# Forming the S3 weight sums of a down projection later, from loads of their own

## The chip, the core and the metric

The kernel runs on one core of a Trainium2 chip. The core has TensorE (matmuls into PSUM), VectorE, ScalarE and GpSimd (elementwise work), and SyncE, whose instruction stream here issues nearly all loads. Each engine works through its own instruction stream in order and waits on semaphores of the others. The metric is the device time of one execution in microseconds (us), the median of several runs.

## The reference

One layer of a decoder trunk over 1024 tokens of width 1024. The layer has three token-mixer branches, an output projection, and a gated MLP; a final RMSNorm closes it. The stage that matters here is the end of the MLP:

```
def _ffn(x, w_gate, w_up, conv_w, conv_b, w_down):
    g = _causal_dwconv(x @ w_gate, conv_w, conv_b)
    return (jax.nn.gelu(g) * (x @ w_up)) @ w_down
...
    x = x + g2[:, None, :] * _ffn(xn, f_wgate, f_wup, f_conv_w, f_conv_b, f_wdown)
return _rmsnorm(x, final_norm)
```

The hidden width of the MLP is 2816 = 22 x 128, so w_down has 2816 rows and 1024 columns. All arrays are float32.

## The kernel before

Every large product is done as a 2 x 2 block product with seven block products in place of eight (the Strassen-Winograd scheme), and every float32 operand is split into two float32r parts, high (`wh`, made by ScalarE) and low (`wl`, made by VectorE or GpSimd as source minus high). A block product is then three matmuls for each pair: high x high, high x low, low x high.

**The gate/up stage** comes before the down stage. For each of 11 pairs k of hidden blocks it makes a gate unit and an up unit of seven products each (line 191 issues their matmuls), loading raw weights into a ring of four buffers (`raw`) and splitting them into rings of eight `wh` and eight `wl` tiles. The convolution and the GELU make `y`, the up unit's evacuation (lines 161 to 172) makes `up`, and `down_tokens` multiplies them and stores the result to `ff_scr`, and four sums of its blocks to `ta_scr` to `td_scr`, from ScalarE's queue (lines 1532 to 1545). The tiles `y`, `up` and `gp` lie in pools that are closed when the stage ends; the pool `sums` with the tiles `held` and `held3`, and the pools `dn` and `last`, are opened in the memory that becomes free.

**The down stage** has seven products, listed in `STEPS`, with 11 rows each: B11 x A11, B21 x A12, ta x S1, tb x S2, B22 x S4, tc x S3, td x A22. A12, A21 and so on are the blocks of w_down and S1 = A21 + A22, S2 = S1 - A11, S3 = A11 - A21, S4 = A12 - S2 its sums. A row is one block of 128 hidden channels: a token tile and a weight tile of 128 x 512, loaded into one `raw` buffer of the same ring (`down_load`: 256 KB each), two splits on ScalarE (`high`), two on VectorE (`low`), and 12 matmuls, three for each of four token tiles (`down_mm`, line 1614). The seven products share PSUM banks in turn and are emptied by `copies` (ScalarE) and `adds` (VectorE). `settle` scales a finished quarter by the gate row `g2b` and adds it to the residual tile `res`; `square` sums its squares on ScalarE.

The order of this stage is written out by hand. `at_slot(s, kind, f)` puts a piece of work at a slot; a slot is one row of a product, so product number si has slots 11 si to 11 si + 10. The pieces are sorted by slot and kind and recorded in this order, and each engine keeps the order of its own instructions. A row's load stands `LD` = 5 slots before its matmuls, its high split `HI` = 3, its low split `LO` = 2; what would fall before slot 0 stands at slot 0. The first two rows are loaded earlier, inside the last gate/up unit (`begun`). How the rows of the down stage interleave with the end of the gate/up stage is decided by a scheduler, which goes by a model of the machine.

The sum S3 is needed in the sixth product only, but A11 is loaded in the first. So row k of the first product also loads A21 into `held3[k]` (line 1670), and `third` (line 1699) subtracts it from the A11 in the raw buffer. The residual tiles `res[t]` are loaded at slots 12 + 2 t, and the second product is settled in the four slots behind it.

Of the kernel before, what the change touches and what calls it, by code (L numbers as in the profile page):

```python
# [16 lines left out]
OP = mybir.AluOpType  # L17
# [8 lines left out]
HALF = 512  # L26
# [43 lines left out]
def trunk(ctx: ExitStack, tc: tile.TileContext, I: dict, out: bass.AP, dbg=None):  # L70
    nc = tc.nc
    pe, act, dve, pool = nc.tensor, nc.scalar, nc.vector, nc.gpsimd
# [20 lines left out]
    def rows_scr(name, n):  # L93
        return [dram.tile([P, S], F32, name=f"{name}{k}_scr") for k in range(n)]
# [6 lines left out]
    x2_scr = rows_scr("x2", NT)  # L101
    ff_scr = rows_scr("ff", KF)
    KH = KF // 2
# [15 lines left out]
    def kview(w, c0, n, r0=0, r1=None):  # L119
        return w[r0:r1, c0:c0 + n].rearrange("(k p) c -> p k c", p=P)  # L120

    def raw_tile(view, shape):
        raw = ring.tile([P] + shape, F32, tag="raw", bufs=4, name="raw")
        nc.sync.dma_start(raw, view)
        return raw
# [7 lines left out]
    def ring_tmp(shape):  # L133
        return ring.tile([P] + shape, F32, tag="st", bufs=3, name="st")
# [458 lines left out]
    for h in range(2):  # L593
        for i in range(4):
            t = 4 * h + i
# [771 lines left out]
    for q in range(4):  # L1367
        raw = raw_tile(kview(I["p_c"], 256 * q, 256, CSPLIT * P, W), [KW - CSPLIT, 256])
# [27 lines left out]
    with ExitStack() as gl_s:  # L1396
# [8 lines left out]
        for h in range(2):  # L1405
# [3 lines left out]
            for c in range(2):  # L1409
                cs = slice(HALF * c, HALF * c + HALF)  # L1410
                pts = [pwo.tile([P, HALF], F32, tag="wo", bufs=4, name="go") for _ in range(4)]
                for k in range(KD):
                    if k % 2 == 0:
                        raw = raw_tile(kview(I["w_out"], HALF * c, HALF, k * P, (k + 2) * P), [2, HALF])
# [10 lines left out]
            for i in range(4):  # L1425
                t = 4 * h + i
# [120 lines left out]
    lo, hi = slice(0, HALF), slice(HALF, D)  # L1547
# [8 lines left out]
    def block_rows(n, k):  # L1556
        r0 = (k + KH * (n[2] == "2")) * P
        return I["f_wdown"][r0:r0 + P, hi if n[1] == "2" else lo]

    def down_load(tn, wn, k, raw=None):  # L1560
        raw = ring.tile([P, 2, HALF], F32, tag="raw", bufs=4, name="raw") if raw is None else raw
        nc.sync.dma_start(raw[:, 0], token_rows(tn, k))
        if wn != "S3":
            nc.sync.dma_start(raw[:, 1], block_rows({"S1": "A21", "S2": "A11", "S4": "A12"}.get(wn, wn), k))
        return raw
# [42 lines left out]
    held, held3 = [[sums.tile([P, HALF], F32, tag=n, bufs=KH, name=n) for _ in range(KH)] for n in ("held", "held3")]  # L1608

    def down_mm(bank, ts_, ws, tp, start):  # L1610
        (th, tl), (wh, wl) = ts_, ws
        sl = slice(tp * P, tp * P + P)
        for j, (a_, b_) in enumerate(((th, wh), (th, wl), (tl, wh))):
            pe.matmul(bank, a_[:, sl], b_, start=(start and j == 0), stop=(j == 2), skip_group_check=True)  # L1614

    def four(bk):
        return [gb3("x") if bk == "x" else gb3("zzww"[tp]) for tp in range(4)]
# [3 lines left out]
    res = [dn.tile([P, D], F32, tag="res", bufs=NT, name="res") for _ in range(NT)]  # L1621
# [5 lines left out]
    LD, HI, LO = 5, 3, 2  # L1627
    todo = []

    def at_slot(s_, kind, f):  # L1630
        todo.append((max(0, s_), kind, f))

    def settle(d, t, sl):

        dve.tensor_tensor(d, d, g2b[:, sl], op=OP.mult)
        dve.tensor_tensor(res[t][:, sl], res[t][:, sl], d, op=OP.add)

    def square(t, dh):
        junk = dn.tile([P, HALF], BF16, tag="junk", bufs=2, name="junk")
        act.activation(junk, res[t][:, (lo, hi)[dh]], AF.Square, scale=1.0 / math.sqrt(D),  # L1640
                       accum_out=ms[t][:, dh:dh + 1])
        if dh == 0:
            pool.tensor_scalar(ms[t][:, 0:1], ms[t][:, 0:1], EPS, None, op0=OP.add)
        else:
            pool.tensor_tensor(ms[t][:, 0:1], ms[t][:, 0:1], ms[t][:, 1:2], op=OP.add)
            pool.tensor_tensor(ms[t][:, 0:1], ms[t][:, 0:1], mhalf[:, :1], op=OP.pow)

    def finish(t):
        for dsl in (lo, hi):
            dve.scalar_tensor_tensor(res[t][:, dsl], res[t][:, dsl], ms[t][:, 0:1], fnb[:, dsl], op0=OP.mult,  # L1650
                                     op1=OP.mult)

    def store(t):
        for dsl in (lo, hi):
            nc.sync.dma_start(out[0, t * P:(t + 1) * P, dsl], res[t][:, dsl])

    def row(si, k, need, slot, alone=False):

        _, tn, wn = STEPS[si]
        it = {}  # L1660

        def load():
            if si == 0 and k < len(begun):
                it["raw"] = begun[k]
            elif alone:
                it["raw"] = down_load(tn, wn, k, lp.tile([P, 2, HALF], F32, tag="lraw", bufs=2, name="lraw"))
            else:
                it["raw"] = down_load(tn, wn, k)
            if wn == "A11":
                nc.sync.dma_start(held3[k], block_rows("A21", k))  # L1670
            if wn == "S1":
                nc.sync.dma_start(held[k], block_rows("A22", k))

        def tile_(tag):
            return lp.tile([P, HALF], F32R, tag="last", bufs=4 * ALONE, name="last") if alone else \
                ring.tile([P, HALF], F32R, tag=tag, bufs=8, name=tag)

        def high():
            raw = it["raw"]
            w = raw[:, 1]  # L1680
            if wn == "S3":
                w = held3[k]
            elif wn in ("S1", "S2", "S4"):
                w = held[k]
                x_, op, y_ = {"S1": (raw[:, 1], OP.add, w), "S2": (w, OP.subtract, raw[:, 1]),
                              "S4": (raw[:, 1], OP.subtract, w)}[wn]
                dve.tensor_tensor(w, x_, y_, op=op)
            it["src"] = raw[:, 0], w
            it["h"] = [tile_("wh") for _ in range(2)]
            for h, src in zip(it["h"], it["src"]):  # L1690
                act.activation(h, src, AF.Copy)  # L1691

        def low():
            it["l"] = [tile_("wl") for _ in range(2)]
            for l, h, src in zip(it["l"], it["h"], it["src"]):
                dve.tensor_tensor(l, src, h.bitcast(F32), op=OP.subtract)  # L1696

        def third():
            dve.tensor_tensor(held3[k], it["raw"][:, 1], held3[k], op=OP.subtract)

        if wn == "A11":
            at_slot(need - LO, 2.5 if need <= LO else 2, third)
        at_slot(need - LD, 0, load)
        at_slot(need - HI, 2, high)
        at_slot(need - LO, 2 if need <= LO else 1, low)
        return lambda: [(h, l) for h, l in zip(it["h"], it["l"])]

    banks, cs = {}, {}
# [22 lines left out]
    for si in range(7):  # L1731
        bk = STEPS[si][0]
        for k in range(KH if si < 6 else KH - ALONE):
            slot = si * KH + k
            get = row(si, k, slot, slot)

            def mm(si=si, bk=bk, k=k, get=get):
                fresh = bk not in banks
                if fresh:
                    banks[bk] = four(bk)  # L1740
                ts_, ws = get()
                for tp in range(4):
                    down_mm(banks[bk][tp], ts_, ws, tp, fresh)

            at_slot(slot, 3, mm)
        if si < 6:
            for tp in range(4):
                at_slot(slot, 5, lambda f=evacs[si], tp=tp: f(tp))
        if si in settled:
            c, t0, dh = settled[si]  # L1750
            for tp in range(4):
                t = t0 + tp
                at_slot(slot + 1 + tp, 4, lambda c=c, tp=tp, t=t, dh=dh: settle(cs[c][tp], t, (lo, hi)[dh]))
                at_slot(slot + 2 + tp, 4, lambda t=t, dh=dh: square(t, dh))
                if dh:
                    at_slot(slot + 3 + tp, 4, lambda t=t: finish(t))
                    at_slot(slot + 4 + tp, 4, lambda t=t: store(t))
    alone = [row(6, KH - ALONE + i, end - 6 + 2 * i, end, True) for i in range(ALONE)]

    def last(tp):  # L1760
# [15 lines left out]
    at_slot(6, 0, lambda: nc.sync.dma_start(g2b, bcast_rows(g_rows[5], P, D)))  # L1776
    at_slot(8, 0, lambda: nc.sync.dma_start(fnb, bcast_rows(I["final_norm"], P, D)))
    for t in range(NT):
        at_slot(12 + 2 * t, 0, lambda t=t: nc.sync.dma_start(res[t], x2_scr[t]))
    for _, _, f in sorted(todo, key=lambda x_: x_[:2]):  # L1780
        f()
    sched2.close()
# [23 lines left out]
```

## Time and profile before

| | us |
|---|---|
| median of 3 runs | 1966.98 (1965.74 to 1968.68) |
| the profiled execution | 1959.93 |
| its span on the core | 1958.1 |
| TensorE busy (matmuls) | 1856.8, 95% of the span |
| VectorE busy | 1295.8, 66% |
| ScalarE busy | 912.8, 47% |
| GpSimd busy | 633.3, 32% |

Times in the profile are counted from the start of the span. A matmul's record overlaps the next one's, so a busy TensorE says only that it did not pause; where it does pause, the rows name the instruction that released it. The granted clock is the share of full speed that TensorE was given. The profile calls the engines PE (TensorE), PEld (its weight loads), DVE (VectorE), ACT (ScalarE), POOL (GpSimd) and SP (SyncE); a q behind the name means the engine's instruction queue, where DMAs are issued.

### The profile page before, as it was taken

The page shows a single profiled execution, that of the slowest core. Times are in us where ns is not written, and L with a number is a line of the kernel's source. Part 1 is how long each engine was busy: PE and PEld are TensorE (multiplying, and loading weights), DVE is VectorE, ACT ScalarE, POOL GpSimd, SP SyncE. Part 2 cuts the span into 40 slices and gives each one's busy share as a digit, 9 for nine tenths or more (in the row PEclk, how much of TensorE's full clock was granted, in tenths as well). Part 3 has the DMA queues.
Part 4 walks back from the last instruction along what each step waited for, and adds up shares of the span by engine and source line. Part 5 has one row for each costly group of instructions (what it writes and reads, how often), then busy time and mean ns, then how long its engine had stood idle before and what let it go on. Part 6 is the DMA issues. An engine that isn't in the chain of part 4 may idle for free.

```text
span 1958.1 us, 26389 instructions
## 1 busy us (share of the span) xinstructions
PE 1856.8 (95%) x9119; PEld 1493.1 (76%) x9119; DVE 1295.8 (66%) x2277; ACT 912.8 (47%) x1689; POOL 633.3 (32%) x1067
## 2 busy tenths in 40 slices
PE   6899998999999999899999999998999999979996
PEld 5677897867777788677777777776888887858885
DVE  5766566556767885555666655579758566667766
ACT  5345456665444444644545433445434343434542
POOL 5320000001311211345656654655545444200001
PEclk9899999999999999899999999999999999989998
DMA  9232423434666768867756256404334333189643
GB/s 322 79 108 100 142 98 129 133 120 156 198 188 198 237 228 250 207 156 177 184 150 164 91 205 214 135 22 140 134 102 130 109 125 101 64 287 324 217 154 121
DMA packets 243078, 313.15 MB, mean 160 GB/s; under 512 B 15991, under 2 KB 166755, under 8 KB 242944
## 3 DMA queue, kind: packets, MB, share of 16 engines
q1 hardware_dynamic: 197520, 186.43, 31.3%
q10 hardware_dynamic: 30384, 75.65, 10.2%
q0 software_dynamic: 15040, 49.38, 9.4%
q8 instruction: 72, 1.18, 0.3%
q14 instruction: 62, 0.51, 0.1%
HBM read 229.47 MB, written 81.93 MB: 159 GB/s over the span
## 4 chain that ended last, share of the span: by engine, by line
PE 78%; DVE 7%; ACT 5%; DMA 4%; issue 3%; POOL 2%; ACTq 0%; SPq 0%; DVEq 0%; POOLq 0%
PE g L298 20%; PE g L191 19%; PE g L1614 10%; PE gp L1158 7%; PE g L337 5%; PE go L1420 4%; PE sl L1225 3%; PE g L215 2%; PE tp L1269 1%; PE o L1298 1%; PE gp L1383 1%; PE o L1301 1%; PE m L790 1%; DVE st L252 1%; ACT wh L254 1%
## 5 line engine op out<-in xcount | busy, mean ns | idle before, releaser
L298 PE MATMUL g<-xs,wh 128*128 128x512 f32 x1344 | 437.7, 407 | 12.0 <-ACT ot L161 12.0
L191 PE MATMUL g<-xs,wh 128*128 128x512 f32 x1176 | 367.9, 394 | 9.5 <-DVE up L168 2.7
L298 PEld LDWEIGHTS g<-xs,wh 128*128 128x128 f32 x1344 | 254.3, 191 | 82.1 <-ACT ot L161 13.7
L298 PE MATMUL g<-xs,wl 128*128 128x512 f32 x672 | 269.1, 400 | 0.0
L191 PEld LDWEIGHTS g<-xs,wh 128*128 128x128 f32 x1176 | 220.5, 188 | 63.0 <-DVE up L168 3.1
L191 PE MATMUL g<-xs,wl 128*128 128x512 f32 x588 | 230.4, 393 | 0.0
L1158 PE MATMUL gp<-oT,wh 128*128 128x512 f32 x512 | 171.6, 415 | 7.3 <-DVE ot L170 3.6
L116 ACT ACTIVATE wh<-raw 128x512 fp32r<-128x512 f32 (+2 forms) x163 | 92.9, 586 | 175.2 <-PE g L191 45.3
L254 ACT ACTIVATE wh<-st 128x512 fp32r<-128x512 f32 x120 | 75.6, 630 | 179.9 <-DVE st L252 179.9
L298 PEld LDWEIGHTS g<-xs,wl 128*128 128x128 f32 x672 | 128.7, 192 | 31.5
L117 POOL TENSOR_TENSOR wl<-st,wh 128x512 fp32r<-128x512 f32 x63 | 101.9, 1618 | 144.7 <-ACT wh L116 139.9
L191 PEld LDWEIGHTS g<-xs,wl 128*128 128x128 f32 x588 | 110.5, 188 | 24.9
L1614 PE MATMUL g<-wh 128*128 128x512 f32 x292 | 114.9, 393 | 14.6 <-ACT wh L1691 14.0
L117 POOL TENSOR_TENSOR wl<-raw,wh 128x512 fp32r<-128x512 f32 (+2 forms) x71 | 92.1, 1298 | 103.0 <-ACT wh L116 100.3
L337 PE MATMUL g<-wh,xs 128*128 128x256 f32 x672 | 124.8, 286 | 0.0
L1614 PE MATMUL g<-wl,wh 128*128 128x512 f32 x292 | 114.9, 393 | 0.6 <-DVE wl L1696 0.6
L1614 PE MATMUL g<-wh,wl 128*128 128x512 f32 x292 | 114.4, 392 | 0.0
L116 ACT ACTIVATE wh<-st 128x512 fp32r<-128x512 f32 x84 | 52.5, 628 | 130.4 <-PE g L191 96.4
L1158 PEld LDWEIGHTS gp<-oT,wh 128*128 128x128 f32 x512 | 89.9, 192 | 30.1 <-issue 7.7
L1691 ACT ACTIVATE wh<-raw 128x512 fp32r<-128x512 f32 x102 | 62.6, 628 | 102.1 <-issue 29.8
L1696 DVE TENSOR_TENSOR wl<-raw,wh 128x512 fp32r<-128x512 f32 x102 | 68.8, 689 | 55.6 <-ACT wh L1691 55.2
L337 PEld LDWEIGHTS g<-wh,xs 128*128 128x128 f32 x672 | 103.8, 188 | 1.6 <-issue 1.4
(331 smaller groups left out, 3922.2 us busy)
## 6 DMA issues: line engine op xcount, KB each, us to landing
raw<-in_w_in_dram SPq DMA_DIRECT2D x66, 512.0 KB, 4.9
raw<-in_f_wdown_dram SPq DMA_DIRECT2D x62, 256.0 KB, 4.3
adaw<-in_w_ada_dram SPq DMA_DIRECT2D x48, 256.0 KB, 5.4
g_scr<-ot ACTq DMA_DIRECT2D x24, 512.0 KB, 3.9
adaw<-in_w_ada_dram POOLq DMA_DIRECT2D x48, 256.0 KB, 4.8
raw<-g_scr SPq DMA_DIRECT2D x24, 512.0 KB, 3.5
qk<-k_scr POOLq DMA_DIRECT2D x24, 512.0 KB, 7.3
raw<-in_f_wgate_dram SPq DMA_DIRECT2D x22, 512.0 KB, 3.8
```

The source lines that it names most:

```text
L116: act.activation(h, src, AF.Copy)
L117: l_eng.tensor_tensor(l, src, h.bitcast(F32), op=OP.subtract)
L191: pe.matmul(banks[bk], a[:, k, :], b, start=(fresh and j == 0), stop=(j == 11), skip_group_check=True)
L254: act.activation(it["h"], bl[name], AF.Copy)
L298: pe.matmul(banks[bk], a[:, k, :], b, start=(fresh and j == 0), stop=(j == 11), skip_group_check=True)
L337: pe.matmul(banks[t2][bk][:, 256 * i:256 * i + 256], a[:, sl], b[:, k % 2, :], start=(fresh and i == 0 and j == 0), stop=(j == 11), skip_g ...
L1158: pe.matmul(pt, a_[:, k % g, :], b_, start=(j == 0), stop=(j == 3 * n - 1))
L1225: pe.matmul(sb[:, of:of + n], lq, kt[:, ks], start=(of == 0 and kt is kh), stop=(kt is kl), skip_group_check=True)
L1420: pe.matmul(pt, a_[:, sl], b_, start=(k == 0 and j == 0), stop=(k == KD - 1 and j == 2))
L1614: pe.matmul(bank, a_[:, sl], b_, start=(start and j == 0), stop=(j == 2), skip_group_check=True)
L1691: act.activation(h, src, AF.Copy)
L1696: dve.tensor_tensor(l, src, h.bitcast(F32), op=OP.subtract)
```

## The change

The subtraction that forms S3, and the load of A21 for it, leave the rows of the first product. A new list of 11 pieces does the same later: `third_load(k)` loads A21 into `held3[k]` and A11 once more into a temporary tile (`ring_tmp`, a ring `st` of three buffers that the gate/up stage used too) at slot 7 + 7k // 5, that is slots 7 to 21, and the subtraction on VectorE stands three slots later. The residual loads stand eight slots later, at 20 + 2 t. The settles and squares of the second product stand 12 slots later, at 34 to 38 in place of 22 to 26.

```diff
-            if wn == "A11":
-                nc.sync.dma_start(held3[k], block_rows("A21", k))
...
-        def third():
-            dve.tensor_tensor(held3[k], it["raw"][:, 1], held3[k], op=OP.subtract)
-
-        if wn == "A11":
-            at_slot(need - LO, 2.5 if need <= LO else 2, third)
...
-                at_slot(slot + 1 + tp, 4, lambda c=c, tp=tp, t=t, dh=dh: settle(cs[c][tp], t, (lo, hi)[dh]))
-                at_slot(slot + 2 + tp, 4, lambda t=t, dh=dh: square(t, dh))
+                at_slot(slot + 1 + tp + 12 * (si == 1), 4, lambda c=c, tp=tp, t=t, dh=dh: settle(cs[c][tp], t, (lo, hi)[dh]))
+                at_slot(slot + 2 + tp + 12 * (si == 1), 4, lambda t=t, dh=dh: square(t, dh))
...
+    a11 = {}
+
+    def third_load(k):
+        a11[k] = ring_tmp([HALF])
+        nc.sync.dma_start(held3[k], block_rows("A21", k))
+        nc.sync.dma_start(a11[k], block_rows("A11", k))
+
+    for k in range(KH):
+        at_slot(10 + 7 * k // 5 - 3, 0, lambda k=k: third_load(k))
+        at_slot(10 + 7 * k // 5, 2, lambda k=k: dve.tensor_tensor(held3[k], a11.pop(k), held3[k], op=OP.subtract))
...
-        at_slot(12 + 2 * t, 0, lambda t=t: nc.sync.dma_start(res[t], x2_scr[t]))
+        at_slot(20 + 2 * t, 0, lambda t=t: nc.sync.dma_start(res[t], x2_scr[t]))
```

The changed lines move instructions on four engines. SyncE's queue, from the load of row 1 (raw_15698) on, before; ff0 to ff10 are the token blocks of the first product:

```order
L1562 DMA raw_15698<-ff1_scr_168 128x512 [waits DMAHW4_49,DMAHW2_49,DVE_49]
L1564 DMA raw_15698<-in_f_wdown_dram 128x512 [waits DMAHW3_49]
L1670 DMA held3_15878<-in_f_wdown_dram 128x512 [waits DMAHW2_49,DMAHW3_49,DMAHW1_49,DMAHW4_49,DMAHW0_49,DMAHW5_49,DVE_49,DMAHW6_49,PE_49,DMAHW7_49,Activation_49,Pool_49]
L1670 DMA held3_15879<-in_f_wdown_dram 128x512
L1562 DMA raw_15911<-ff2_scr_169 128x512 [waits Pool_49]
L1564 DMA raw_15911<-in_f_wdown_dram 128x512
L1670 DMA held3_15880<-in_f_wdown_dram 128x512
L1562 DMA raw_15915<-ff3_scr_170 128x512
```

And in the changed kernel, from the same load on:

```order
L1562 DMA raw_15698<-ff1_scr_168 128x512 [waits DMAHW4_49,DMAHW2_49,DVE_49]
L1564 DMA raw_15698<-in_f_wdown_dram 128x512 [waits DMAHW3_49]
L1562 DMA raw_15909<-ff2_scr_169 128x512 [waits DMAHW5_49,DVE_49]
L1564 DMA raw_15909<-in_f_wdown_dram 128x512 [waits DMAHW6_49]
L1562 DMA raw_15912<-ff3_scr_170 128x512 [waits DMAHW7_49,DMAHW3_49,DVE_49]
L1564 DMA raw_15912<-in_f_wdown_dram 128x512 [waits DMAHW4_49]
L1562 DMA raw_15915<-ff4_scr_171 128x512 [waits DMAHW1_49,DMAHW6_49,DMAHW0_49,DVE_49]
```

The load of held3's first tile, which waits for every engine and DMA lane, stood ahead of rows 2 and later; now it stands behind row 12's load.

TensorE's stream around the last group of the gate/up stage (g3_15746) in the changed kernel; wh_15930 is row 1, wh_15938 row 2. Before, this group stood directly behind row 1:

```order
L1614 MATMUL g3_15952<-wh_15930,wl_15933 128x512
L1614 MATMUL g3_15949<-wh_15938,wh_15937 128x512
L1614 MATMUL g3_15949<-wl_15942,wh_15937 128x512 [waits DVE_49]
L1614 MATMUL g3_15949<-wh_15938,wl_15941 128x512
L1614 MATMUL g3_15950<-wh_15938,wh_15937 128x512
L1614 MATMUL g3_15950<-wl_15942,wh_15937 128x512
L1614 MATMUL g3_15950<-wh_15938,wl_15941 128x512
L1614 MATMUL g3_15951<-wh_15938,wh_15937 128x512
L191 MATMUL g3_15746<-xs_12374,wh_15823 128x512 [waits DVE_49]
```

Seven matmuls of row 2 moved ahead of the group.

ScalarE's stream in the last up unit of the changed kernel; raw_15909 is row 2, raw_15912 row 3, raw_15915 row 4. Before, none of these splits stood there; the first of them came behind the stores of L1532 to L1545:

```order
L165 ACTIVATE up_15540<-g3_15705 128x512 [waits PE_49]
L1689 ACTIVATE wh_15938<-raw_15909 128x512 [waits DMAHW6_49,PE_49,Activation_49]
L1525 ACTIVATE y_15693<-y_15693 128x1024 [waits DVE_49]
L1525 ACTIVATE y_15694<-y_15694 128x1024 [waits DVE_49]
L1689 ACTIVATE wh_15945<-raw_15912 128x512 [waits DMAHW3_49,PE_49,Pool_49]
L167 ACTIVATE up_15541<-g3_15705 128x512 [waits DMAHW7_49,PE_49]
L1689 ACTIVATE wh_15946<-raw_15912 128x512 [waits DMAHW4_49,PE_49,Activation_49]
L1689 ACTIVATE wh_15972<-raw_15915 128x512 [waits DMAHW6_49,PE_49,Activation_49]
L1532 DMA ff21_scr_188<-up_15541 128x1024 [waits DVE_49]
```

The splits of rows 2 to 4 moved in among the up unit's evacuations, one of them directly ahead of L167.

## Rows read from the trace of the kernel before

**Rows 1.** The page's slices: the span in 40 equal parts, TensorE and traffic.

```profile
PE   6899998999999999899999999998999999979996
GB/s 322 79 108 100 142 98 129 133 120 156 198 188 198 237 228 250 207 156 177 184 150 164 91 205 214 135 22 140 134 102 130 109 125 101 64 287 324 217 154 121
```

**Rows 2.** Windows of 10 us: length, busy time of five engines, clock, DMA share, GB/s.

```profile
1700.00:1710.00 10.00, 10.00 (x45) 8.26 (x44) 6.65 (x7) 4.68 (x6) 0.00 (x0) 1.00 0.00 0
...
1720.00:1730.00 10.00, 0.00 (x0) 0.00 (x0) 3.84 (x6) 0.00 (x0) 0.00 (x0) 0.58 0.63 216
1730.00:1740.00 10.00, 6.74 (x18) 5.07 (x19) 6.26 (x10) 3.77 (x6) 0.00 (x0) 0.57 0.83 268
1740.00:1750.00 10.00, 10.00 (x46) 8.27 (x45) 8.60 (x14) 5.63 (x9) 0.00 (x0) 1.00 1.03 380
1750.00:1760.00 10.00, 10.00 (x46) 8.29 (x45) 7.99 (x13) 6.67 (x12) 0.00 (x0) 1.00 1.04 393
1760.00:1770.00 10.00, 10.00 (x46) 8.28 (x45) 4.56 (x8) 5.70 (x10) 0.00 (x0) 1.00 0.98 358
1780.00:1790.00 10.00, 10.00 (x46) 8.26 (x45) 7.08 (x12) 4.16 (x8) 0.00 (x0) 1.00 0.98 357
...
1810.00:1820.00 10.00, 10.00 (x46) 8.29 (x45) 8.62 (x14) 5.85 (x11) 0.00 (x0) 1.00 0.90 307
```

**Rows 3.** TensorE's waits from 1690 to 1950: total us, times, longest.

```profile
PE g L1614 <- ACT wh L1691: 14.0, 1, 14.0
PE g L1614 <- ACT up L167: 0.7, 1, 0.7
```

**Rows 4.** TensorE's instructions: start, us, instruction, count, idle time before and its end.

```profile
1718.92 0.39 PE L191 MATMUL g<-xs,wl 128*128 128x512 f32 x1
1733.26 0.79 PE L1614 MATMUL g<-wh 128*128 128x512 f32 x1 [13.96 <-ACT wh L1691]
...
1738.42 0.47 PE L1614 MATMUL g<-wh,wl 128*128 128x512 f32 x1
1738.73 0.40 PE L1614 MATMUL g<-wh 128*128 128x512 f32 x1
```

**Rows 5.** Waits of SyncE's queue from 1600 to the end.

```profile
SPq L1562 <- DVE wl L1696: 96.0, 57, 5.2
SPq L1670 <- DMA ff_scr<-up: 49.9, 2, 44.1
```

**Rows 6.** The chain that ended last, in order of time: start, us, what.

```profile
1723.98 2.70 DMA td_scr<-y
...
1726.76 0.33 SPq L1670
...
1733.26 179.54 PE g L1614 x779
```

**Rows 7.** VectorE's instructions that read the raw buffers for the last time.

```profile
1681.81 0.69 DVE L148 TENSOR_TENSOR st<-raw,st 128x512 f32<-128x512 f32 x1 [1.87 <-POOL wl L117]
...
1689.60 0.69 DVE L117 TENSOR_TENSOR wl<-raw,wh 128x512 fp32r<-128x512 f32 x1
...
1697.11 0.68 DVE L1696 TENSOR_TENSOR wl<-raw,wh 128x512 fp32r<-128x512 f32 x1
```

**Rows 8.** DMA issues from 1725 to 1760: count, KB each, median us to landing.

```profile
raw<-ff_scr SPq DMA_DIRECT2D x16, 256.0 KB, 5.3
raw<-in_f_wdown_dram SPq DMA_DIRECT2D x15, 256.0 KB, 5.5
```

**Rows 9.** ScalarE's copy L167 in the last up unit.

```profile
1712.24 0.60 ACT L167 ACTIVATE up<-g 128x512 f32<-128x512 f32 x1 [1.31 <-PE g L191]
```

**Rows 10.** One turn of the down stage's loop on ScalarE, VectorE and SyncE.

```profile
1768.66 1.15 ACT L1691 ACTIVATE wh<-raw 128x512 fp32r<-128x512 f32 x2 [1.57 <-PE g L1614]
1769.33 1.29 DVE L1696 TENSOR_TENSOR wl<-raw,wh 128x512 fp32r<-128x512 f32 x2 [1.42 <-ACT wh L1691]
1770.65 0.32 SPq L1562 DMA_DIRECT2D raw<-ff_scr  x1
1771.01 0.43 SPq L1564 DMA_DIRECT2D raw<-in_f_wdown_dram  x1
```

## The prediction, made before the result was known

> **What bounds the kernel now.** I read the slices of the page first, then the stretch that looked odd in windows of 10 us, then who waited for whom there, and last the chain that ended last. In the slices the reader is to see that TensorE is nearly full between the first and the last slice, except in slice 36 of 40, where its digit is 7, next to the highest traffic of the program (324 GB/s) [rows 1]. In windows this is the start of the down stage: between 1720 and 1730 us TensorE executes nothing, between 1730 and 1740 it is busy for 6.74 us with a granted clock of 0.57, and from 1740 on it never pauses [rows 2]. The waits name it: one wait of 14.0 us of TensorE for ScalarE's split of a loaded row, and only 0.7 us of another kind beside it [rows 3]. The instructions give the exact size: the last matmul of the gate/up stage starts at 1718.92, the next one at 1733.26, and twelve matmuls from there stand further apart than later [rows 4].
>
> Why did the split wait? Its row had not been loaded, and SyncE's queue shows why: it stood 44.1 us behind one DMA of L1670, the load of A21 into held3 [rows 5]. That load writes into memory that the gate/up stage's y and up tiles had held, so it waits for their last stores; in the chain its issue follows at once on the td_scr store at 1726.7 [rows 6]. All loads of rows 2 to 10 stood behind it, though they need nothing of that memory. After the start the chain is 779 matmuls of L1614 without a gap [rows 6]. So what is lost before 1733 is lost at the end of the program, as long as nothing later waits longer.
>
> **The change part by part.** A slot is one row of the down stage: 12 matmuls. From 1738.73 on the chain's matmuls take (1733.26 + 179.54 - 1738.73) / 767 = 0.227 us each [rows 4, 6], so a slot is 2.72 us.
>
> *What goes.* The held3 loads leave the head of SyncE's queue. Rows 2 and 3 then need only free buffers of the raw ring, which the last up unit releases: its S4 sum at 1681.81 + 0.69 and its A22 split at 1689.60 + 0.69 [rows 7]. So they can be issued at about 1682.5 and 1690.3, and with the 5.5 us to landing that the loads took while the DMA engines were full [rows 8] they are there by 1696, long before TensorE comes to them; 1700 to 1710 had no DMA traffic at all [rows 2]. Row 4 follows when row 0 is split (1697.11 + 0.68 [rows 7]). What that removes:
> - the idle stretch, 1733.26 - (1718.92 + 0.227) = 14.11 us;
> - the slow matmuls behind it: 12 in 1738.73 - 1733.26 = 5.47 us where 12 x 0.227 = 2.72 would do, so 2.75 us. They run at the lower of the two clocks (1.2 GHz) after an idle stretch; without it there is no reason for the clock to fall.
>
> *What is late next.* I followed the new order through the last up unit by these durations. The order moves a piece of row 2 ahead of the last L191 group, and on ScalarE row 3's first split stands ahead of L167, the copy that frees a PSUM bank for the fourth part of row 0. Both wait for the same L191 group, so L167 ends about 0.6 us (one ScalarE pass [rows 9]) later than 1712.84, and the matmul that waited 0.7 us for it waits some 1.25 us: a loss of 0.55 us. Behind it: row 0's rest, row 1 and 7 matmuls of row 2 (22 in all) to 1718.5, the last L191 group to 1721.2, row 2's rest to 1722.3, then row 3, 4, 5. Row 5's last split, on the buffer that the last L191 group frees at 1721.2, ends near 1722.5 and is wanted at 1727.7; rows 6 and 7 have their loads by 1720 and their splits by 1728, and are wanted at 1730.4 and later. Row 3 starts at 1722.3 instead of 1738.73: 16.4 us, the same as 14.11 + 2.75 - 0.55 = 16.3.
>
> *What is added.* Eleven loads of A11, 256 KB each, and the eleven of A21 moved from the first slots to slots 7 to 21. On SyncE an issue takes 0.32 to 0.43 us [rows 10] and the queue mostly waits for VectorE's splits [rows 5], so 11 more cost nothing there. The eleven subtractions are the same ones as before, 0.69 us each on VectorE, moved from slots 0 to 10 into slots 10 to 24, where VectorE was busy for 4.56 us of 10 in the window from 1760 [rows 2] and the settles of the second product (two passes a tile) have left: nothing, as long as their loads are there. The third-last of them (row 8) now stands directly ahead of the four adds that empty the PSUM banks which the third product needs; by the loop below it ends about as TensorE delivers the first of these, with some 1 us to spare. The residual loads go to slots 20 to 34 and are first wanted at slot 34, 14 slots on. The settles and squares of the second product go to slots 34 to 37: for those four slots VectorE has five passes (about 3.2 us by the pace of [rows 7]) a slot of 2.72 us, a backlog of 2 us against splits that are made two slots, 5.4 us, ahead.
>
> *The unknown is the DMA traffic of slots 7 to 27.* The rows there need 13.9 MB, the new pairs 5.8 MB, four residual tiles 2.1 MB and the broadcast norm row 0.5 MB: 22.3 MB in 21 x 2.72 = 57.2 us, 390 GB/s. The windows show up to 393 GB/s at a full share, 358 with residual tiles in the mix, and 307 in the slowest window with a share of 0.90 [rows 2]. What lateness can be borne is in the loop: ScalarE starts a split when TensorE frees its buffer (1768.66), VectorE is done with it at 1770.62 and the load into the freed raw buffer goes out at 1770.65 [rows 10]. That load is for a row whose own split starts four slots after 1768.66, so it has 10.9 - 2.0 = 8.9 us to land, 3.4 more than the 5.5 us seen; and a split that ends 2 us after its start is used three slots after it, so 6.2 us more pass before TensorE waits. Together 9.5 us. Adding up slot by slot what is asked and what a rate delivers, the loads fall behind by at most 3.1 us at 393 GB/s and 5.8 us at 358: hidden. At 307 it is 16.8 us, so a stall of 7.3 us, with one slow start of 2.75 us about 10. I take the value nearest to the rows with a share of 0.98 and above, which is nothing, and keep 10 for the range. A gain from this part is excluded, since it only adds bytes.
>
> On this the rows show 380 and 393 GB/s over 10 us each, on one core [rows 2]. The Trainium skill (DMA: Bandwidth & Descriptors, Specifications) gives a limit of about 358 GB/s for one core from HBM. By that figure the loads would be 5.8 us late at most and the sum would still be 16.3; by the rows the limit lies higher. It speaks against the change in one way: it leaves 3.7 us of cover and not 6.4.
>
> **Sum.** 14.11 + 2.75 - 0.55 = 16.3 us. Against the profiled execution, 1959.9 us (span 1958.1 and 1.8 around it), that gives 1943.6. The median of the timed runs, 1967.0, lies 7.0 above the profiled one, spread over what the trace can't show, so I subtract the same from it: 1950.7 us.
>
> **The rivals.**
> 1. *The loads of slots 7 to 27 come late.* For it: the 390 GB/s asked is what the fullest windows gave, and held3's subtractions stand in VectorE's order ahead of splits and of the adds that free PSUM banks. Against it: before, these engines moved 358 to 393 GB/s with TensorE never waiting [rows 2, 3]. At 307 GB/s the gain is 16.3 - 10 = 6.2 us: about 1961.
> 2. *The wait only changes its place (the change doesn't do what it says).* Now the g2b load and the first A21 load carry the wait for the freed memory, and loads of later rows stand behind them. For it: SyncE's order. Against: they stand behind the loads of rows 11 and 12, which go out when rows 7 and 8 are split, at about 1728 and 1731, when the last L191 group is over and the last store (2.7 us after its issue [rows 6]) lands by 1732. For no change at all row 13's load would have to be 9.5 + 16 us late. 1967.
> 3. *Slower.* The mechanism of rival 1 with a lower rate: TensorE ends up going at the pace of the DMA engines between slot 7 and slot 30. The price reaches the gain when the loads fall behind by 16.3 - 2.75 + 9.5 = 23 us, which by the same adding up is at about 285 GB/s; at 265 GB/s they are 30.8 us late, a stall of 21.3 + 2.75 against 16.3: 8 us slower, 1975. For it: the residual tiles and the token blocks already pulled the rate from 393 to 357 and below [rows 2]. Against: the windows under 330 GB/s have a share under 0.95, so part of their low rate is that less was asked.
>
> **How the numbers follow.** Forecast 0.74 (1947 to 1955: the 0.55 may not occur, or a few us of rival 1 may), rival 1 0.13, rival 2 0.06, rival 3 0.07. Outside of 1946.5 to 1961 I leave rivals 2 and 3 and the far part of rival 1, under 2 in 10. A measurement of this kernel tells about 0.2%, 3.9 us, from no change: faster below 1963 holds the forecast and nearly all of rival 1, 0.86; within it 0.07; slower 0.07.
>
> **What would show it.** Right: no wait of TensorE over 2 us at the start of the down stage, granted clock 1.00 there, SyncE's 44 us wait gone from ahead of row 2's load and that load issued before 1695, and row 3's first matmul near 1722. The wait for L167 near 1.2 us shows the small loss. Wrong in the second half: waits of TensorE for VectorE's or ScalarE's splits, or a clock under 1.00, between 1733 and 1800, with VectorE waiting for DMA of held3 or st ahead of them. If the idle stretch is still there with another name behind it, rival 2 holds; if the start is gapless and the end of the program has not moved by 16 us, the chain after 1900 has become the bound, which I count at nothing because it starts from the last rows' matmuls.

## The result and the profile after

| | before | after |
|---|---|---|
| median of 3 runs, us | 1966.98 (1965.74 to 1968.68) | 1946.43 (1944.83 to 1948.49) |
| ratio after / before | | 0.9896 [0.9873, 0.9918] |
| profiled execution, its span, us | 1959.93, 1958.1 | 1948.49, 1946.8 |

The changed kernel is 20.6 us faster by these medians, 16.5 us by the traces (below), where 16.3 was forecast. Two timings of the kernel before in the first set of experiments below, 2292.76 and 3031.69 us at a granted clock of 0.75 and 0.56, are left out of the ratios. Line numbers have moved: ScalarE's split is now L1689, VectorE's split L1694, the sums S1, S2 and S4 L1685, the new S3 subtraction L1760, its two loads L1755 and L1756, the adds that empty PSUM banks L1717, the last settle L1770 and L1771.

The slices of the page, TensorE and traffic as in [rows 1]:

```profile
PE   6899999999999999899999999999999999999996
GB/s 317 85 109 101 143 99 121 143 120 149 188 194 186 241 235 231 228 161 174 171 150 166 112 203 171 138 57 138 112 120 150 99 98 119 119 234 388 247 156 121
```

The digit 7 of slice 36 is gone. The traffic of that slice fell from 287 to 234 GB/s, and that of the next one rose from 324 to 388.

Windows of 10 us over the start of the down stage, with the columns of [rows 2] (length; busy time of TensorE, its weight loads, VectorE, ScalarE, GpSimd; clock, DMA share, GB/s):

```profile
1710.00:1720.00 10.00, 8.97 (x40) 7.09 (x39) 8.08 (x10) 6.88 (x11) 0.00 (x0) 1.00 0.32 105
1720.00:1730.00 10.00, 10.00 (x46) 8.29 (x45) 7.17 (x10) 3.39 (x6) 0.00 (x0) 1.00 0.58 188
...
1740.00:1750.00 10.00, 10.00 (x46) 8.29 (x45) 5.38 (x9) 5.70 (x11) 0.00 (x0) 1.00 1.04 388
...
1760.00:1770.00 10.00, 10.00 (x46) 8.29 (x45) 6.21 (x10) 4.62 (x8) 0.00 (x0) 1.00 1.05 386
...
1800.00:1810.00 10.00, 10.00 (x46) 8.29 (x45) 8.16 (x13) 6.61 (x12) 0.00 (x0) 1.00 1.04 393
```

TensorE is full from 1720 on and its clock stays at 1.00. From 1740 to 1810 the DMA engines have no time to spare: share 1.04 or 1.05 and 386 to 393 GB/s in all seven windows.

TensorE's waits from 1690 to 1950 (total us, times, longest), for [rows 3]:

```profile
PE g L1614 <- ACT up L167: 1.0, 1, 1.0
PE g L1614 <- DVE wl L1694: 0.6, 1, 0.6
```

The wait of 14.0 us for the split is gone, the one for L167 grew from 0.7 to 1.0. Two instructions of TensorE, for [rows 4], the first matmul behind that wait and the first one of row 3:

```profile
1718.47 0.50 PE L1614 MATMUL g<-wh 128*128 128x512 f32 x1 [1.03 <-ACT up L167]
...
1727.44 0.39 PE L1614 MATMUL g<-wh 128*128 128x512 f32 x1
```

SyncE's queue from 1600 on, for [rows 5]; the row of 44.1 us is absent. Of waits for the last stores of the gate/up stage these are left, a token block's load and the first A21 load of the new list:

```profile
SPq L1562 <- DMA ff_scr<-up: 4.6, 1, 4.6
...
SPq L1755 <- DMA td_scr<-y: 1.3, 1, 1.3
```

SyncE's issues: the loads of rows 2 and 3, then g2b and the first A21 load of the new list.

```profile
1687.77 0.33 SPq L1562 DMA_DIRECT2D raw<-ff_scr  x1
...
1695.49 0.33 SPq L1562 DMA_DIRECT2D raw<-ff_scr  x1
...
1735.25 0.39 SPq L1779 DMA_DIRECT2D g2b<-g_scr  x1
...
1738.01 0.33 SPq L1755 DMA_DIRECT2D held<-in_f_wdown_dram  x1
```

The loads of rows 2 and 3 go out 32 to 34 us before TensorE wants the rows. In the chain that ended last, the down stage is one piece from row 0's rest on, for [rows 6]:

```profile
1718.47 5.28 PE g L1614 x22
1723.75 2.72 PE g L191 x12
1726.47 175.00 PE g L1614 x772
```

**A ruler for the rest.** The stages ahead of the down stage take more or less time from execution to execution, with the same instructions. The loads of L1562 in the window 1640 to 1760 show it (count, duration in ns, first and last start), first of before:

```profile
L1562 SPq DMA_DIRECT2D raw<-ff_scr x18: 320/327/432, 1663.2 to 1759.8; - x18
```

and of after:

```profile
L1562 SPq DMA_DIRECT2D raw<-ff_scr x21: 326/327/389, 1668.4 to 1758.3; - x21
```

Row 0's load starts 5.2 us later in the changed kernel's profiled execution, so all its times above stand 5.2 us later than they would in that of before. From this load to the end of the span it is 1958.1 - 1663.2 = 294.9 us before and 1946.8 - 1668.4 = 278.4 after: 16.5 us. This distance repeated to 0.1 us where a kernel's profile was taken again (the change three times, e9's kernel twice), while the start of row 0's load went from 1663.2 to 1671.9 in the fourteen traces of this case. So a loss in the down stage is read by this ruler, and the timed medians, which carry the spread of the earlier stages, say whether it agrees.

### The profile page after: what moved, and what is told of

Its sections match the earlier page's. It is cut to its first block, busy times and chain, and to the rows that moved or that the text cites. A ratio compares the mean times of both kernels' runs of the same rounds, so it can differ in the third digit from the quotient of the medians.

```text
span 1946.8 us, 26418 instructions
## 1 busy us (share of the span) xinstructions
PE 1859.5 (96%) x9119; PEld 1497.0 (77%) x9119; DVE 1291.9 (66%) x2277; ACT 912.1 (47%) x1689; POOL 636.0 (33%) x1067
## 5 line engine op out<-in xcount | busy, mean ns | idle before, releaser
L191 PE MATMUL g<-xs,wh 128*128 128x512 f32 x1176 | 367.9, 394 | 9.4 <-DVE up L168 2.7
L191 PEld LDWEIGHTS g<-xs,wh 128*128 128x128 f32 x1176 | 220.4, 188 | 62.9 <-DVE up L168 3.1
L191 PE MATMUL g<-xs,wl 128*128 128x512 f32 x588 | 230.4, 393 | 0.0
L191 PEld LDWEIGHTS g<-xs,wl 128*128 128x128 f32 x588 | 110.5, 188 | 24.9
L1233 ACT ACTIVATE pm<-pm,stat 128x128 f32<-128x128 f32 (+1 forms) x192 | 88.8, 464 | 32.5 <-DVE stat L1230 29.2
L1158 PE MATMUL gp<-oT,wl 128*128 128x512 f32 x256 | 102.8, 401 | 0.0
```

The source lines that it names most:

```text
L191: pe.matmul(banks[bk], a[:, k, :], b, start=(fresh and j == 0), stop=(j == 11), skip_group_check=True)
L1158: pe.matmul(pt, a_[:, k % g, :], b_, start=(j == 0), stop=(j == 3 * n - 1))
L1233: act.activation(pm[:, of:of + n], pm[:, of:of + n], AF.Exp, scale=-1.0, bias=stt[:, cfg, 0, idx:idx + 1], accum_out=stt[:, cfg, 1, idx:id ...
```

## The experiments

| run | median us (lowest to highest, runs) | ratio to before [95%] | row 0's load to end, us |
|---|---|---|---|
| before | 1964.86, 1964.55, 1964.27 in the three sets | | 294.9 |
| e1, the change again | 1947.97 (1946.43 to 1951.33, 6) | 0.9917 [0.9903, 0.9930] | 278.4 |
| e15, the change a third time | 1949.13 (1943.30 to 1951.43, 6) | 0.9919 [0.9903, 0.9935] | 278.3 |
| e3, residual and settles later, S3 as before | 1965.11 (1962.27 to 1972.54, 12) | 1.0004 [0.9992, 1.0016] | 294.9 |
| e4, one A21 load first | 1964.72 (1962.33 to 1970.25, 10) | 1.0000 [0.9987, 1.0012] | 294.5 |
| e6, one A21 load behind row 5 | 1952.75 (1952.02 to 1956.71, 4) | 0.9941 [0.9926, 0.9956] | 285.9 |
| e2, S3 move alone | 1953.15 (1949.56 to 1958.68, 6) | 0.9944 [0.9927, 0.9961] | 285.1 |
| e12, residual loads early | 1950.80 (1948.78 to 1954.35, 6) | 0.9934 [0.9919, 0.9948] | 284.8 |
| e7, eleven more loads | 1955.26 (1953.06 to 1955.93, 4) | 0.9948 [0.9933, 0.9963] | 287.4 |
| e8, pairs in calm slots | 1945.73 (1944.55 to 1949.71, 4) | 0.9905 [0.9890, 0.9920] | 278.4 |
| e9, tail interleaved | 1944.50 (1942.34 to 1947.10, 4) | 0.9897 [0.9880, 0.9913] | 273.3 |
| e14, tail interleaved again | 1940.85 (1940.74 to 1944.01, 5) | 0.9888 [0.9871, 0.9905] | 273.3 |
| e13, calm slots and tail | 1941.16 (1939.34 to 1946.14, 5) | 0.9887 [0.9869, 0.9904] | 273.3 |

e1 to e4 ran on one chip as a first set, e6 to e9 as a second, e12 to e15 as a third. The last column is each profiled execution's span minus the start of row 0's load.

### The size: the change again (e1, e15)

No edit.

> The changed kernel itself, timed beside the kernel before in five rounds. First theory (the gain is the idle stretch of 14.1 us and its slow matmuls, less a later L167): 16.5 us faster, so a difference of 15.5 to 17.5 us; the 20.6 us of the first three runs had 4 us of scatter from the stages ahead. Rival (something beside the start of the down stage became faster too): 19 to 22 us.

> The changed kernel once more, as the partner of the three others on this chip. Theory: 16 to 17 us below the kernel before, a wait of TensorE of about 1.0 us for ScalarE's copy at the start of the down stage and none over 1.5 us after it. Rival: 20 us, as in the first comparison.

They are 16.9 and 15.1 us faster than the before of their sets; the second lies a little under the 16 to 17 us expected. By the ruler it is 16.5 or 16.6 us in all three profiled executions of the change. The first comparison's 20.6 us held some 4 us of the earlier stages' spread: e1's profiled execution took 1951.33 us with row 0's load at 1671.2, e15's 1943.30 with it at 1663.2; both differ by 8.0.

### One load put back (e4, e6)

The change, with the A21 load for held3's first tile alone moved ahead of row 2's loads (e4) or behind row 5's (e6). The traffic stays the same.

```diff
-        nc.sync.dma_start(held3[k], block_rows("A21", k))
+        if k:
+            nc.sync.dma_start(held3[k], block_rows("A21", k))
...
+    at_slot(0, -1, lambda: nc.sync.dma_start(held3[0], block_rows("A21", 0)))
```

This is e4; in e6 the -1 of the last line is 0.5.

> The changed kernel with a single load moved: that of held3's first tile stands again at the head, ahead of row 2's loads; the ten others, the A11 loads and the sums stay late. First theory (SyncE's queue waits there for the last stores out of the memory that held3 takes): the idle stretch is back with 13 to 15 us and slow matmuls behind it, and 15 to 17 us of the gain are gone, so about the time of the kernel before. Rival (what counts is the traffic taken out of the start, 11 loads of 256 KB or 7.3 us at 393 GB/s): one load of 0.7 us, so at most 1 us lost.

> As the run with one load first, but held3's first load stands behind row 5's loads in SyncE's queue instead of ahead of row 2's. First theory (the loads behind it wait for the last stores, which end some 10 us after the last gate/up matmul): rows 2 to 5 are there, row 6 is not; TensorE runs out after row 5 and waits 6 to 10 us, so 8 to 12 us of the gain are lost with the slow matmuls. Rival (traffic at the start): at most 1 us lost.

With the one load in front the whole gain is gone. TensorE's waits in e4:

```profile
PE g L1614 <- ACT wh L1689: 13.1, 1, 13.1
```

and SyncE's (L1759 is the moved load):

```profile
SPq L1759 <- DMA ff_scr<-up: 50.0, 2, 44.3
```

That is the 14.0 and the 44.1 us of before [rows 3, 5] almost to the us, made by 256 KB. TensorE's order at the end of the gate/up stage changed back too (row 2 stands behind the last L191 group again). But row 2's load went out at 1730.84 in e4, and at 1687.77 in the changed kernel's execution, so in no order could row 2 have been multiplied before. So the stall came from the place of a load that waits for freed memory, not from the eleven loads' bytes. Behind row 5 it is seen from SyncE and TensorE in e6:

```profile
SPq L1759 <- DMA ff_scr<-up: 21.3, 1, 21.3
```

```profile
1741.12 0.79 PE L1614 MATMUL g<-wh 128*128 128x512 f32 x1 [4.65 <-ACT wh L1689]
...
1744.44 0.40 PE L1614 MATMUL g<-wl,wh 128*128 128x512 f32 x1
```

The queue stands half as long, the wait comes back at a third, and seven matmuls behind it take 1744.44 - 1741.12 = 3.32 us where 1.59 would do. By the ruler 7.5 us are lost (285.9 - 278.4); what the wait and the slow matmuls leave of them is mostly a second pause of 0.8 us later on, for the adds at L1717. The direction is as expected, wait and loss are somewhat smaller.

### The two parts apart (e3, e2, e12)

e3 is before with the later residual loads and settles only; e2 is the change without them; e12 is the change with the residual loads alone back where they were.

```diff
-                at_slot(slot + 1 + tp + 12 * (si == 1), 4, lambda c=c, tp=tp, t=t, dh=dh: settle(cs[c][tp], t, (lo, hi)[dh]))
-                at_slot(slot + 2 + tp + 12 * (si == 1), 4, lambda t=t, dh=dh: square(t, dh))
+                at_slot(slot + 1 + tp , 4, lambda c=c, tp=tp, t=t, dh=dh: settle(cs[c][tp], t, (lo, hi)[dh]))
+                at_slot(slot + 2 + tp , 4, lambda t=t, dh=dh: square(t, dh))
...
-        at_slot(20 + 2 * t, 0, lambda t=t: nc.sync.dma_start(res[t], x2_scr[t]))
+        at_slot(12 + 2 * t, 0, lambda t=t: nc.sync.dma_start(res[t], x2_scr[t]))
```

This is e2. e12 is its last two lines alone, and e3 the whole in reverse, made in the kernel before.

> Residual loads eight slots and settles 12 slots later, the S3 sums as before. First theory: no change, within 1 us, with the 14 us wait for the split at the start of the down stage still there. Rival (the shift brings the 4 us that the first result shows over 16.5): 3 to 5 us faster.

> The S3 sums alone moved as in the change; residual loads and the second product's settles where they were before. First theory: the same gain as the whole change, 16 us, within 1 us of it; the residual tiles then add to the fullest slots (17 to 22), whose loads fall some 3 us further behind, within the 9.5 us of cover. Rival (the later residual loads and settles are what makes the S3 traffic bearable, or bring something by themselves): 3 us or more less than the whole change.

> The changed kernel with the residual loads back at slots 12 + 2 t; the settles of the second product stay 12 slots later. This splits the shift that the run with the S3 move alone undid as a whole. Theory (traffic): four residual tiles of 512 KB between slots 12 and 20 put the loads of the S1 and S3 sums about 3 us further behind, and the adds of the third product's start stand behind these sums: a wait of TensorE for the adds of 3.5 to 5 us near 1780, some ten slow matmuls behind it, and about 1952 to 1954, some 5 us over the change, the same as with the S3 move alone. Rival (VectorE's passes): the settles were what made VectorE late; then no wait over 1.5 us here and the time of the change, about 1947.

The shift by itself does nothing (e3: ratio 1.0004, the 13.9 us wait still there). But without it the S3 move gives 9.8 us in place of 16.5 by the ruler, so e2's rival was right. TensorE at the start of the third product in e2, the last matmul before the pause and the slow ones behind it:

```profile
1782.33 0.39 PE L1614 MATMUL g<-wh,wl 128*128 128x512 f32 x1
1787.15 0.76 PE L1614 MATMUL g<-wh 128*128 128x512 f32 x1 [4.43 <-DVE c L1717]
...
1791.13 0.57 PE L1614 MATMUL g<-wh 128*128 128x512 f32 x1
1791.54 0.40 PE L1614 MATMUL g<-wl,wh 128*128 128x512 f32 x1
```

The pause is 1787.15 - (1782.33 + 0.227) = 4.6 us, and ten matmuls take 4.39 us in place of 2.27: together 6.7, the ruler's 285.1 - 278.4. TensorE waited for the adds that free its PSUM banks. Why they were late stands directly ahead of them on VectorE, in e2:

```profile
1785.12 0.69 DVE L1685 TENSOR_TENSOR held<-raw,held 128x512 f32<-128x512 f32 x1 [2.05 <-DMA held<-in_f_wdown_dram]
1785.72 0.68 DVE L1760 TENSOR_TENSOR held<-st,held 128x512 f32<-128x512 f32 x1
1786.33 2.47 DVE L1717 TENSOR_TENSOR c<-c,g 128x512 f32<-128x512 f32 x4
```

and in the changed kernel the same three:

```profile
1775.85 0.69 DVE L1685 TENSOR_TENSOR held<-raw,held 128x512 f32<-128x512 f32 x1 [0.18 <-DMA held<-in_f_wdown_dram]
1776.45 0.68 DVE L1760 TENSOR_TENSOR held<-st,held 128x512 f32<-128x512 f32 x1
1777.28 2.73 DVE L1717 TENSOR_TENSOR c<-c,g 128x512 f32<-128x512 f32 x4
```

The adds wait for no DMA themselves. They stand behind an S1 sum (L1685) that does, and that belongs to a row three slots on. In e12, with the settles late and only the residual loads early, the same wait is there, seen from VectorE and from TensorE:

```profile
1777.13 0.69 DVE L1685 TENSOR_TENSOR held<-raw,held 128x512 f32<-128x512 f32 x1 [2.10 <-DMA held<-in_f_wdown_dram]
```

```profile
1779.17 0.77 PE L1614 MATMUL g<-wh 128*128 128x512 f32 x1 [3.96 <-DVE c L1717]
```

and the ruler gives 284.8: 6.4 of the 6.7 us. So it is the traffic of the residual loads in slots 12 to 20 and not the settles' passes on VectorE; that rival falls but for 0.3 us. Its median, 1950.8, missed the 1952 to 1954 expected and is only 1.7 above e15: medians of six runs between 1943 and 1954 do not show this difference, the traces of one execution each do.

### How much lateness is borne (e7, e8)

e7 adds a load of 256 KB that nothing reads to each of the eleven pairs; e8 moves the pairs to slots 29 + 2 k, the sums three slots behind them, and puts residual loads and settles back where they stood before the change.

In e7, inside `third_load`:

```diff
+        for _ in range(1):
+            nc.sync.dma_start(lp.tile([P, HALF], F32, tag="idle", bufs=4, name="idle"), block_rows("A12", k))
```

In e8, beside the edit of e2:

```diff
-        at_slot(10 + 7 * k // 5 - 3, 0, lambda k=k: third_load(k))
-        at_slot(10 + 7 * k // 5, 2, lambda k=k: dve.tensor_tensor(held3[k], a11.pop(k), held3[k], op=OP.subtract))
+        at_slot(29 + 2 * k, 0, lambda k=k: third_load(k))
+        at_slot(32 + 2 * k, 2, lambda k=k: dve.tensor_tensor(held3[k], a11.pop(k), held3[k], op=OP.subtract))
```

> The changed kernel with one more load of 256 KB (A12 into a tile that nothing reads) behind each of the eleven pairs: it adds 2.9 MB to slots 7 to 21 and no other work. Theory of the DMA traffic, as the run with the S3 sums alone taught it (the loads fall behind; the S1 load on VectorE's path ahead of the adds of the second product is late; these adds free PSUM banks): by the same adding up at 388 GB/s the loads are 7.8 us late at slot 21, against 2.6 in the changed kernel and 5.9 with the S3 sums alone, where TensorE waited 4.4 us; so a wait of 5 to 8 us at that place and, with slow matmuls, 7 to 10 us lost. The prediction's cover of 9.5 us: nothing lost.

> The A21 and A11 pairs loaded at slots 29 to 49 and the S3 sums made at slots 32 to 52, where the DMA engines are half idle; residual loads and settles where they were in the kernel before. If the later residual loads and settles serve only to make room for the pairs in slots 7 to 27: the whole gain of the change, 16 to 17 us, with no wait of TensorE over 1.5 us and a DMA share under 1.0 in most windows. Rival (the early residual loads or settles hinder the start by themselves): 3 us or more less than the change.

e7's S1 sum ahead of the adds, TensorE's restart behind them, and VectorE's waits from 1735 to 1850:

```profile
1781.56 0.69 DVE L1685 TENSOR_TENSOR held<-raw,held 128x512 f32<-128x512 f32 x1 [1.53 <-DMA held<-in_f_wdown_dram]
```

```profile
1783.60 0.77 PE L1614 MATMUL g<-wh 128*128 128x512 f32 x1 [5.99 <-DVE c L1717]
```

```profile
DVE held L1685 <- DMA held<-in_f_wdown_dram: 9.7, 7, 2.7
```

In the changed kernel VectorE's wait there is 3.4 us in all and 1.1 at the longest. It is the same stall as in e2, and the ruler shows 9.0 us lost. Adding up slot by slot what is asked and what 388 GB/s delivers, as the prediction did, the loads are behind at slot 21 by an estimated 2.6 us in the change, 5.9 in e2 and e12, and 7.8 in e7; TensorE waits 0, 4.4 and 4.0, and 6.0 us. These estimates put the runs in the right order, but how late the sum itself is can be read from the traces. The third product is due one matmul (0.227 us) behind the last one of the second product, which starts at 1782.33 in e2, 1774.82 in e12 and 1777.22 in e7. In the changed kernel the third product starts without a pause:

```profile
1779.12 0.39 PE L1614 MATMUL g<-wh 128*128 128x512 f32 x1
```

| run | S1 sum starts | third product due | sum against due | TensorE pauses, us |
|---|---|---|---|---|
| the change | 1775.85 | 1779.12 | 3.27 ahead | 0 |
| e12 | 1777.13 | 1775.05 | 2.08 behind | 4.12 |
| e2 | 1785.12 | 1782.56 | 2.56 behind | 4.59 |
| e7 | 1781.56 | 1777.45 | 4.11 behind | 6.15 |

In all three runs the pause is 2.0 us longer than the sum is behind. So the sum has to start 2.0 us ahead of the third product, the change has 3.27 - 2.04 = 1.2 us to spare, and each us beyond that comes through. In e8, with nothing extra in these slots, VectorE waits for TensorE at the adds and no longer for a load:

```profile
DVE c L1717 <- PE g L1614: 1.0, 1, 1.0
```

The ruler gives 278.4, the full gain, with residual and settles in their old places: all that their shift does in the change is make room for the pairs.

### The tail (e9, e14, e13)

The trace after showed a second stretch, unchanged by the change: some 17 us from the last matmul to the end. The last group of matmuls in the changed kernel (start, us):

```profile
1918.77 11.04 PE L1614 MATMUL g<-last 128*128 128x512 f32 x48
```

It ends at 1929.81, the span at 1946.8. The chain there, one turn of four:

```profile
1926.27 0.61 DVE c L1770
1926.90 0.70 DVE res L1771
1927.69 0.73 ACT junk L1640 x2
...
1928.49 0.20 POOL ms L1645
...
1928.76 0.56 POOL ms L1646
1929.35 1.41 DVE res L1650 x2
1930.76 0.61 DVE c L1770
```

VectorE's scaling of a tile (L1650) waits for ScalarE's squares and GpSimd's root, and the next tile's settle stands behind it: 4.49 us a turn. The edit records a tile's scaling and store behind the next tile's settle:

```diff
-        finish(tp)
-        store(tp)
+        for t in {0: (), 3: (2, 3)}.get(tp, (tp - 1,)):
+            finish(t)
+            store(t)
```

> The changed kernel with the four last token tiles' finish and store recorded one tile later, so that VectorE takes the next tile's settle before it waits for the norm of the one before (the chain of waits ends with four turns of 4.5 us behind matmuls that come 2.7 us apart). Expected if that chain sets the end: about 5 us faster than the change, the last matmul at the same distance from the start of the stage. Rival (the stores' landing sets the end): 0 to 1 us.

> The change with finish and store of the last four tiles recorded one tile later, a second time, beside the change on the same chip. Theory: 4 to 5 us below the change, as the traces of the tail have it. Rival: no more than 1 us below it.

> The pairs at slots 29 + 2 k, residual loads and settles where they stood before the change, and finish and store of the last four tiles recorded one tile later. Theory: the two edits touch stretches that lie 60 us apart, so the tail is 5 us shorter (12 us from the last matmul to the end in place of 17), no new wait of TensorE at the start of the stage, and about 1941 to 1944. Rival: what the trace shows of the tail does not reach the timed runs, and the time is that of the calm slots alone, about 1946.

The chain in e14, where a turn is VectorE's own work, 2.7 us:

```profile
1921.68 0.70 DVE c L1770
...
1922.41 0.69 DVE res L1771
1923.10 1.32 DVE res L1650 x2
1924.42 0.68 DVE c L1770
```

The ruler gives 273.3 in all three: 5.1 us less than the change. e14 and e13 are 8.3 and 8.0 us below the change's median in their set, which holds some of the spread. The calm slots add nothing on top, as the ruler says. e14 and e13 are the fastest of this case, some 23 us below before by the medians and 21.6 by the ruler.

## Why the prediction was right, and where it was not

- *The idle stretch and the slow matmuls, 14.11 + 2.75 us.* Right: both are gone, the clock is 1.00, and e4 brings the wait back with one load.
- *The start of rows 2 and 3.* Right: loads forecast at 1682.5 and 1690.3; 1687.77 and 1695.49 less 5.2 are 1682.6 and 1690.3. Row 3's first matmul, forecast at 1722.3, came at 1727.44 - 5.2 = 1722.2.
- *The later L167.* Right in place; the wait is 1.03 us where 1.25 was forecast, so it costs 0.33 and not 0.55. That is the 0.2 us between 16.3 and 16.5.
- *The wait that might change its place (rival 2).* No: the g2b and the first A21 load went out at 1735.25 and 1738.01, behind the loads of rows 11 and 12; the A21 load waited 1.3 us for the td_scr store, and TensorE did not wait for what came after.
- *The traffic of slots 7 to 27.* The rate was right: 386 to 393 GB/s for 70 us. On this the Trainium skill (DMA: Bandwidth & Descriptors, Specifications) gives about 358 GB/s for one core, as half of what two cores share; one core alone moved more in the windows here, and they decide.
- *"Together 9.5 us" of cover.* This step failed, and the result only hid it. It followed a late load to the row's own matmuls, which are three slots behind the sum. But S1's sum has its load five slots and itself three slots ahead of its matmuls, 2 x 2.72 = 5.4 us apart, against the 5.5 us to landing [rows 8]: by the slots nothing is to spare. Behind the sum on VectorE stand the adds that TensorE wants at once. The text saw them ("some 1 us to spare") and did not carry that into the cover. By its sum 9.5 - 3.1 = 6.4 us would be left to the change at 393 GB/s; the traces of e2, e12 and e7 show 1.2. Nor is its "hidden" for up to 5.8 us of lateness borne out: e2, where the same adding up at 388 GB/s has the loads at most 6.6 us late (an estimate), lost 6.7 us. That the change just fits at the rate that came is luck, as far as this step goes.
- *Residual loads and settles, costed at nothing.* Right alone (e3), wrong as a part: beside the pairs in slots 7 to 21, 6.7 of the 16.5 us are lost without the shift, nearly all by the loads (e12). The sum held only because all parts came together.
- *The level, 1950.7.* The first median, 1946.43, came 4.3 lower, just under the lower end of the range (1946.5 to 1961). Two medians of three runs carry the spread of the earlier stages: over more runs before stands at 1964.3 to 1964.9, and 16.3 us less is 1948.0 to 1948.6, with 1947.97 and 1949.13 measured in e1 and e15. So the gain was right, and the level it was taken from too high.

What stays open is whether the stall at the adds goes if the A21 loads need no freed memory at all or if the adds stand ahead of the sum; neither was tried. Nor is it shown what makes the stages before row 0's load vary by 8.7 us. Of the 8.0 us between e1 and e15 some 5 arise from 790 to 1320 us, where the granted clock differs in some windows (900 to 1000: 0.97 and 1.00).

## What to carry to other kernels

On an in-order queue one load whose destination waits for freed memory holds back every load behind it, so such loads go behind those that need nothing. When traffic is added to a full stretch, follow a late load not to its own consumer but to whatever stands behind that consumer on its engine; the cover is what the most urgent of these has: here 1.2 us were left where the loop seemed to leave 6.4. And measure a local change from a fixed point inside the trace: from row 0's load the down stage repeated to 0.1 us, while whole executions spread by 8.

## What the runs showed of the hardware

- One core alone moved 386 to 393 GB/s for 70 us in loads of 256 KB, with matmuls at full pace.
- A pause of 1.03 us left the granted clock at 1.00; after one of 4.43 us (e2) the window 1780 to 1790 had a mean of 0.73, and ten matmuls came slowly, most of them 0.427 us apart in place of 0.227; after 4.65 us (e6) it was seven, after 13.96 us (before) twelve. The slow start costs 1.73 us in e6, 2.1 in e2 and 2.75 before: it does not grow in step with the pause.
